# Taking even and odd chunks in turns in two small matrix products of an RWKV-7 block

## The chip, the cores and the metric

The kernel runs on one NeuronCore of a Trainium2 chip. The metric is the device time of one execution in microseconds (us). The kernel before was run three times: 3058.14, 3070.52 and 3070.98 us, with a median of 3070.52 us. A further execution, recorded by the hardware profiler, is what the profile below describes.

The engines are called as the profile calls them: PE is the matrix engine (PEld its weight loads), DVE the vector engine, ACT the scalar engine, POOL the GpSimd engine, SP the one that issues the DMAs. PSUM is the memory that PE writes its products into. A "stationary" operand is loaded into the array, a "moving" one streams through it.

## The reference: what is computed

A decoder block for 2048 tokens of width 1024 with two parallel branches, a causal convolution and RWKV-7 time mixing with 16 heads of width 64. The part that matters here is the RWKV-7 state, one 64 x 64 matrix a head, updated token by token:

```
def step(state, inp):
    r_t, w_t, k_t, v_t, kk_t, b_t = inp
    sk = jnp.einsum('bhvk,bhk->bhv', state, kk_t)
    state = (state * w_t[:, :, None, :] - sk[..., None] * b_t[:, :, None, :]
             + v_t[..., None] * k_t[:, :, None, :])
    return state, jnp.einsum('bhvk,bhk->bhv', state, r_t)
...
o = _rwkv7_scan(r, decay.reshape(hd), k, v, kk, kk * a)
o = _layernorm(o, gn_g.reshape(RWKV_HEADS, RWKV_HEAD), gn_b.reshape(RWKV_HEADS, RWKV_HEAD), GN_EPS)
```

Around it stand an input projection of width 9344, the convolution branch, two branch projections, sigmoid gates, an output projection and a final RMSNorm.

## The kernel before

**Tiling and stages.** The sequence is cut into 4 blocks (b) of 512 tokens. For each block the 16 heads are taken in 4 groups (g) of 4 heads; a group is two pairs (q) of two heads (hh). So there are 16 groups in all. The first 2531 us or so of the profile are these groups, with the input projections, the gates and the convolution laid between their steps; after that come the branch projections and the output.

**Chunks.** Inside a group the 512 tokens are cut into 8 chunks (c) of 64 tokens. A chunk's parity e = c % 2 decides which partitions its data live in, so that two chunks share one tile: `vrow(e)` is partitions 0 to 63 for an even chunk and 64 to 127 for an odd one, `prow(e)` the other half. `kcol` is `prow` and `rcol` is `vrow`. For each chunk and head the matrix `As` holds the products of keys and queries (L537, masked at L539); `uv` holds the values in the rows `vrow(e)`, and later the solved updates in the rows `prow(e)`.

**A group, in the source's order.**
- The two `pair` generators make decay factors, keys, queries and values (PE lines L505, L537, L552, L570; most of the rest of PE's time is the projections at L205).
- The values' part of x (L589 to L600): for each half c4 of the chunks (four chunks), a PSUM tile `aux` receives `As` times `uv` for four chunks and four heads. The stationary operand is 64 rows by 64 columns of `As`, the moving one 64 rows by 64 columns of `uv`, the output lies in the partitions `prow(e)`. Two copies on ACT (L600) move it to `XO`.
- The triangular inverse: blocks of `As` go to DRAM and come back as `La`, POOL makes the inverse in 31 steps (L624, L626), and it goes by DRAM back into `As`. DVE transposes parts of it (L652) for the products at L656 and L665.
- The recurrence over the 8 chunks: L683, L685 on DVE, L688 (four products of one chunk, 64 by 64, all in the partitions of that chunk's parity), L690 on DVE, L694, and L698 on DVE, which makes the next state.
- The last products of o (L700 to L713): again for each c4 a PSUM tile `late`, of which there is one, receives `As` times `uv` for four chunks and four heads. Here the stationary operand has all 128 rows and 64 columns, and the output lies in the partitions `vrow(e)`. These products are issued after the recurrence's last product. Two adds on DVE (L713) move the tile into `XO`.
- The normalisation of o and its store (L725 to L742). `XO` has one buffer.

**The order of the work.** The kernel is written with a tile framework that places semaphores, and lays out each engine's instructions with a simulated timeline (`schedule_with_timeline_sim=True`). The source's order gives the priority. So the last products of one group and the values' part of the next stand close together in PE's order, with projections between.

**How a product is recorded.** The operands are fp32, and the trace has two weight loads and two matmuls for each product written in the source; they are called passes here. At L596 and L708 there are 512 products each and 1024 passes.

**Another line of the same shape.** L505 (in `pair`) multiplies squared keys with columns of ones: for c in 0 to 7, a stationary operand of 128 rows by 64 columns and a moving one of 2 columns, into the partitions `prow(c % 2)`. Its parity changes with each product.

Of the kernel before, what the change touches and what calls it, by code (L numbers as in the profile page):

```python
# [82 lines left out]
def hybrid_block(ctx: ExitStack, tc: tile.TileContext, x, vecs, convk, w2a2, final_g, ada, w_in, w_co, w_ro, w_o, crow, out,  # L83
# [365 lines left out]
    def prow(e):  # L449
        return slice(64, 128) if e == 0 else slice(0, 64)  # L450

    def vrow(e):
        return slice(0, 64) if e == 0 else slice(64, 128)
# [121 lines left out]
    def group(b, g, h, lora, fill):  # L575
# [11 lines left out]
        for e in range(2):  # L587
            nc.gpsimd.memset(XO[vrow(e), e::2], 0.0)
        heads = [(q, hh) for q in range(2) for hh in range(2)]  # L589
        for c4 in range(NCH // 4):  # L590
            pv = pa.tile([P, 2, 2, P], F32, name="aux", tag="aux")
            for c in range(4 * c4, 4 * c4 + 4):
                e = c % 2
                for q, hh in heads:
                    hs = slice(64 * hh, 64 * hh + 64)
                    nc.tensor.matmul(pv[prow(e), c // 2 % 2, q, hs], As[q][vrow(e), hh, c, kcol(e)], uv[vrow(e), c, q, hs],  # L596
                                     start=(c // 2 % 2 == 0 and q == 0 and hh == 0), stop=(c // 2 % 2 == 1 and q == 1 and hh == 1),
                                     skip_group_check=True)
            for e in range(2):
                nc.scalar.copy(XO[prow(e), 4 * c4 + e:4 * c4 + 4:2], pv[prow(e)])  # L600
# [73 lines left out]
        for c in range(NCH):  # L674
            cc, e = c // 2, c % 2
# [25 lines left out]
        for c4 in range(NCH // 4):  # L701
            po = pl.tile([P, 2, 2, P], F32, name="late", tag="late")
            with tc.issue_after(last.ins if hasattr(last, "ins") else last):
                for c in range(4 * c4, 4 * c4 + 4):
                    e = c % 2
                    for q, hh in heads:
                        hs = slice(64 * hh, 64 * hh + 64)
                        nc.tensor.matmul(po[vrow(e), c // 2 % 2, q, hs], As[q][:, hh, c, rcol(e)], uv[:, c, q, hs],  # L708
                                         start=(c // 2 % 2 == 0 and q == 0 and hh == 0), stop=(c // 2 % 2 == 1 and q == 1 and hh == 1),
                                         skip_group_check=True)  # L710
            for e in range(2):
                sl = slice(4 * c4 + e, 4 * c4 + 4, 2)
                nc.vector.tensor_tensor(out=O[vrow(e), 2 * c4:2 * c4 + 2], in0=po[vrow(e)], in1=XO[vrow(e), sl], op=ALU.add)  # L713
# [158 lines left out]
    for b in range(NB):  # L872
        h = hprep(b) if b else hprep0(x0, ada_steps())
        lora = lora_split(h)
        for g in groups:
# [29 lines left out]

            wcount[0] = WSH
            group(b, g, h, lora, fill)
            if b == 0 and g == GG:
                for _ in ada_cols(srow, l3, "As", ASB, [((16 + k, 17 + k), (hgate_col[:, k:k + 1], hgate_col[:, k + 1:k + 2]))
# [247 lines left out]
```

## Time and profile before

| What | Value |
|---|---|
| Median of three runs | 3070.52 us |
| Lowest, highest | 3058.14, 3070.98 us |
| The profiled execution | 3056.37 us |
| Its span | 3054.7 us |
| Its mean granted clock of PE | 0.982 |
| Busy: PE, DVE, POOL, ACT | 95%, 67%, 41%, 33% |
| HBM traffic over the span | 226 GB/s |
| PE busy at L596, at L708 | 47.3, 49.8 us |

How to read it. A row of the groups by line gives line, engine, operation, `out<-in`, the array's rows and columns that are used (64*64), the moving operand's shape, the count, then the busy time in us and the mean duration of one instruction in ns, and after the second bar the idle time of the engine just before them with what ended it. A row of the timeline gives start and length in us of a run of like instructions, with the idle time before it in brackets. Ends of matmuls are modelled, and matmuls overlap, so the pace is read from starts: the length of a run less the length of one pass, over the number of steps. A row of the busy time by stretch gives the stretch, its length, then busy time and count of PE, PEld, DVE, ACT and POOL, the granted clock, the share of the DMA engines and GB/s. A row of the waits gives who waited for whom, us in total, times, and the longest.

### The profile page before, as it was taken

The page shows a single profiled execution, that of the slowest core. Times are in us where ns is not written, and L with a number is a line of the kernel's source. Part 1 is how long each engine was busy: PE and PEld are TensorE (multiplying, and loading weights), DVE is VectorE, ACT ScalarE, POOL GpSimd, SP SyncE. Part 2 cuts the span into 40 slices and gives each one's busy share as a digit, 9 for nine tenths or more (in the row PEclk, how much of TensorE's full clock was granted, in tenths as well). Part 3 has the DMA queues.
Part 4 walks back from the last instruction along what each step waited for, and adds up shares of the span by engine and source line. Part 5 has one row for each costly group of instructions (what it writes and reads, how often), then busy time and mean ns, then how long its engine had stood idle before and what let it go on. Part 6 is the DMA issues. An engine that isn't in the chain of part 4 may idle for free.

```text
span 3054.7 us, 64810 instructions
## 1 busy us (share of the span) xinstructions
PE 2911.1 (95%) x25672; PEld 2754.0 (90%) x25672; DVE 2045.2 (67%) x3879; ACT 1010.8 (33%) x1887; POOL 1257.3 (41%) x1788
## 2 busy tenths in 40 slices
PE   6789998999999999999999999999999999899998
PEld 5789898999999998999999998999999978687988
DVE  6676877686766675767677667667689534767333
ACT  4424344433333242324242424232332112333101
POOL 3445455533443435243434355426276004555000
PEclk9999999999999999999999999999999999999999
DMA  8666757774747477648585888646457687989674
GB/s 300 220 233 199 250 198 260 242 236 152 243 142 257 140 248 239 194 139 273 161 276 168 274 276 271 199 157 204 154 184 243 199 277 281 325 294 339 235 277 171
DMA packets 366367, 697.14 MB, mean 228 GB/s; under 512 B 135984, under 2 KB 154736, under 8 KB 366064
## 3 DMA queue, kind: packets, MB, share of 16 engines
q1 hardware_dynamic: 366064, 693.00, 67.9%
q8 instruction: 202, 3.31, 0.5%
q14 instruction: 101, 0.83, 0.1%
HBM read 504.04 MB, written 187.70 MB: 226 GB/s over the span
## 4 chain that ended last, share of the span: by engine, by line
PE 57%; DMA 15%; DVE 12%; POOL 7%; ACT 3%; issue 3%; SPq 2%; DVEq 0%; ACTq 0%; POOLq 0%
PE ps_main L205 40%; DMA w_st<-w_in_t 3%; PE aux L537 3%; DVE acc L774 2%; POOL TT L626 2%; POOL itmp L624 2%; DMA w_gr<-grow_d 2%; DMA w_st<-w_co_t 2%; PE xo L688 2%; PE pout L1078 2%; PE pout L1079 2%; PE pout L1077 2%; DMA w_st<-w_ro_t 1%; PE xo L683 1%; PE xo L694 1%
## 5 line engine op out<-in xcount | busy, mean ns | idle before, releaser
L205 PE MATMUL ps_main<-h_hi,w_hi 128*128 128x256 f32 x4608 | 953.4, 285 | 24.3 <-ACT w_hi L188 16.1
L205 PE MATMUL ps_main<-h_hi,w_lo 128*128 128x256 f32 x4608 | 955.6, 285 | 9.6 <-POOL w_lo L190 6.5
L205 PE MATMUL ps_main<-h_lo,w_hi 128*128 128x256 f32 x4608 | 953.4, 284 | 0.0
L205 PEld LDWEIGHTS ps_main<-h_hi,w_hi 128*128 128x128 f32 x4608 | 718.8, 190 | 33.7 <-ACT w_hi L188 17.3
L205 PEld LDWEIGHTS ps_main<-h_hi,w_lo 128*128 128x128 f32 x4608 | 718.2, 190 | 18.3 <-POOL w_lo L190 7.7
L205 PEld LDWEIGHTS ps_main<-h_lo,w_hi 128*128 128x128 f32 x4608 | 717.7, 190 | 4.8 <-issue 0.2
L774 DVE SCALAR_TENSOR_TENSOR acc<-u,ck,acc 128x512 f32<-128x512 f32 x928 | 698.0, 752 | 19.4
L624 POOL TENSOR_TENSOR itmp<-La,TT 128x126 f32<-128x126 f32 (+22 forms) x496 | 181.9, 367 | 126.7 <-DMA La<-dA 91.1
L626 POOL TENSOR_TENSOR TT<-TT,itmp 128x126 f32<-128x126 f32 (+22 forms) x496 | 190.1, 383 | 36.6
L190 POOL TENSOR_TENSOR w_lo<-w_st,w_hi 128x1024 fp32r<-128x1024 f32 x47 | 113.1, 2407 | 116.5 <-ACT w_hi L188 94.6
L680 ACT ACTIVATE Se<-S,pe 128x128 f32<-128x128 f32 x256 | 89.0, 395 | 198.0 <-DVE S L698 196.9
L537 PE MATMUL aux<-KR,BKz 128*128 128x128 f32 x1024 | 137.9, 283 | 12.4 <-POOL KR L523 6.2
L698 DVE TENSOR_TENSOR S<-xo,Se 64x128 f32<-64x128 f32 x256 | 73.5, 287 | 107.6 <-PE xo L694 96.9
L537 PEld LDWEIGHTS aux<-KR,BKz 128*128 128x128 f32 x1024 | 126.9, 197 | 14.9 <-POOL KR L523 6.8
L188 ACT CAST w_hi<-w_st 128x1024 fp32r<-128x1024 f32 x71 | 74.3, 1047 | 195.9 <-DMA w_st<-w_in_t 159.3
L690 DVE TENSOR_TENSOR uv<-xo,rn 64x256 f32<-64x256 f32 x128 | 53.8, 421 | 103.0 <-PE xo L688 101.6
L539 DVE TENSOR_TENSOR As<-aux,maskA 128x512 f32<-128x512 f32 x128 | 87.3, 687 | 38.4 <-PE aux L537 37.3
L685 DVE TENSOR_TENSOR XO<-xo,XO 128x256 f32<-128x256 f32 x128 | 53.7, 419 | 86.1 <-PE xo L683 70.1
L560 POOL TENSOR_TENSOR vv<-rk,vv 128x512 f32<-128x512 f32 x32 | 43.9, 1372 | 154.3 <-ACT rk L559 148.0
L754 ACT ACTIVATE th<-ps_main 128x512 f32<-128x512 f32 x64 | 38.1, 596 | 206.8 <-PE ps_main L205 150.1
L531 ACT COPY BKz<-BK 64x512 f32<-64x512 f32 x128 | 78.9, 616 | 62.7 <-PE aux L537 39.7
L786 ACT ACTIVATE th<-ps_main 128x512 f32<-128x512 f32 x64 | 38.1, 595 | 182.8 <-PE ps_main L205 172.7
(301 smaller groups left out, 5530.9 us busy)
## 6 DMA issues: line engine op xcount, KB each, us to landing
w_hi<-kh_in SPq DMA_DIRECT2D x219, 512.0 KB, 4.2
w_lo<-kl_in SPq DMA_DIRECT2D x219, 512.0 KB, 5.4
w_st<-w_in_t SPq DMA_DIRECT2D x73, 512.0 KB, 4.7
kh_in<-w_hi SPq DMA_DIRECT2D x71, 512.0 KB, 2.9
kl_in<-w_lo SPq DMA_DIRECT2D x71, 512.0 KB, 4.8
w_hi<-kh_ro SPq DMA_DIRECT2D x32, 512.0 KB, 5.1
w_lo<-kl_ro SPq DMA_DIRECT2D x32, 512.0 KB, 6.1
w_hi<-kh_co SPq DMA_DIRECT2D x32, 512.0 KB, 3.9
```

What stands on the lines that cost most here:

```text
L188: nc.scalar.copy(hi, st)
L190: lo_eng.tensor_tensor(out=lo, in0=st, in1=hi.bitcast(F32), op=ALU.subtract)
L205: nc.tensor.matmul(ps[:, qs], ww[:, k, :], aa[k][:, qs], start=(k == 0 and t == 0 and q == 0), stop=(k == KT - 1 and t == 2 and q == ms - ...
L531: nc.scalar.copy(BKz[hs, hh], BK[hs, c4 * 2:c4 * 2 + 2])
L537: nc.tensor.matmul(pA[:, c // 2, es], BKz[:, hh, c // 2, es], KR[:, cc, es], start=(c == 0), stop=(c == 3), skip_group_check=True)
L539: nc.vector.tensor_tensor(out=Asb[:, hh, c4 * 4:c4 * 4 + 4, :].rearrange("p (a e) n -> p a (e n)", e=2), in0=pA, in1=flat(maskA).unsqueeze ...
L624: nc.gpsimd.tensor_tensor(out=tmp[:, :ni, :nt], in0=La[:, j:j + 1, j + 1:].broadcast_to([P, ni, nt]), in1=TT[:, :ni, j:j + 1].broadcast_to ...
L626: nc.gpsimd.tensor_tensor(out=TT[:, :ni, j + 1:], in0=TT[:, :ni, j + 1:], in1=tmp[:, :ni, :nt], op=ALU.add)
L680: nc.scalar.mul(Se[:, q, :], Sg[:, q, :], R[q]["pe"][:, c:c + 1])
L688: nc.tensor.matmul(xo[pr_, q, hs], As[q][pr_, hh, c, kcol(e)], XO[pr_, c, q, hs], start=(q == 0 and hh == 0), stop=(q == 1 and hh == 1), s ...
L698: nc.vector.tensor_tensor(out=Sg[hs, :, hs], in0=xo[hs, 2:4, hs], in1=Se[hs, :, hs], op=ALU.add)
L774: nc.vector.scalar_tensor_tensor(out=acc if i + 1 < HALO else yj, in0=u[:, i:i + TB], scalar=ck[:, j, i:i + 1], in1=acc, op0=ALU.mult, op1 ...
```

## The change

In both places the four chunks of a PSUM tile were taken one after the other, each with its four heads. Now they are taken in two couples, an even chunk with the next odd one, and within a couple each head's product of the even chunk is followed by the same head's product of the odd chunk. The products themselves, their operands and their places are the same, and so are the conditions that start and stop the sums in PSUM.

```
+
+        def turns(c4):
+            return [(4 * c4 + 2 * a + e, q, hh) for a in range(2) for q, hh in heads for e in range(2)]
+
         for c4 in range(NCH // 4):
             pv = pa.tile([P, 2, 2, P], F32, name="aux", tag="aux")
-            for c in range(4 * c4, 4 * c4 + 4):
-                e = c % 2
-                for q, hh in heads:
+            for c, q, hh in turns(c4):
+                    e = c % 2
                     hs = slice(64 * hh, 64 * hh + 64)
                     nc.tensor.matmul(pv[prow(e), c // 2 % 2, q, hs], As[q][vrow(e), hh, c, kcol(e)], uv[vrow(e), c, q, hs],
                                      start=(c // 2 % 2 == 0 and q == 0 and hh == 0), stop=(c // 2 % 2 == 1 and q == 1 and hh == 1),
...
             with tc.issue_after(last.ins if hasattr(last, "ins") else last):
-                for c in range(4 * c4, 4 * c4 + 4):
-                    e = c % 2
-                    for q, hh in heads:
+                for c, q, hh in turns(c4):
+                        e = c % 2
                         hs = slice(64 * hh, 64 * hh + 64)
                         nc.tensor.matmul(po[vrow(e), c // 2 % 2, q, hs], As[q][:, hh, c, rcol(e)], uv[:, c, q, hs],
```

## The prediction

> **What bounds the kernel now.** I read the page first, then the groups by line, then the timeline around the two edited places, then the waits and the busy time by stretch. The page:
>
> ```profile
> span 3054.7 us, 64810 instructions
> PE 2911.1 (95%) x25672; PEld 2754.0 (90%) x25672; DVE 2045.2 (67%) x3879; ACT 1010.8 (33%) x1887; POOL 1257.3 (41%) x1788
> PE 57%; DMA 15%; DVE 12%; POOL 7%; ACT 3%; issue 3%; SPq 2%; DVEq 0%; ACTq 0%; POOLq 0%
> ```
>
> PE is busy for 95% of the span and idle for 143.6 us of it. PE time that is really saved should therefore mostly show in the end. The groups by line, with x products recorded as two passes each (16 groups of 8 chunks of 4 heads are 512 products, and the rows say x1024):
>
> ```profile
> L688 PE MATMUL xo<-XO,As 64*64 64x64 f32 x1024 | 90.0, 226 | 4.9 <-DVE XO L685 2.3 <-DVE carry L438 2.0 <-DVE As L670 0.6
> L708 PE MATMUL late<-uv,As 128*64 128x64 f32 x1024 | 49.8, 230 | 3.6 <-DVE XO L713 3.6
> L596 PE MATMUL aux<-uv,As 64*64 64x64 f32 x1024 | 47.3, 226 | 1.8 <-ACT tk L571 1.8
> L505 PE MATMUL aux<-bones,sq 128*64 128x2 f32 x512 | 23.3, 202 | 4.2 <-ACT sq L501 4.2
> ```
>
> The two edited lines, L596 (the values' part) and L708 (the last products of o), hold 97.1 us of PE. They are 3% of the span, so no gain can be large. What they could shrink to is read from how runs of them lie in time:
>
> ```profile
> 258.40 0.63 PE L505 MATMUL aux<-bones,sq 128*64 128x2 f32 x16
> 265.32 0.68 PE L688 MATMUL xo<-XO,As 64*64 64x64 f32 x8
> 292.18 1.54 PE L708 MATMUL late<-uv,As 128*64 128x64 f32 x32
> 296.27 2.69 PE L596 MATMUL aux<-uv,As 64*64 64x64 f32 x64 [1.77 <-ACT tk L571]
> ```
>
> One pass of these lasts 0.20 us at L505 and 0.22 us at the others (medians of 198, 218 and 222 ns, below). Taking that off a row's length gives the time from the first start to the last:
>
> ```profile
> L505 PE MATMUL aux<-bones,sq x512: 197/198/268, 73.4 to 2286.0; 128*64 128x2 f32 x171
> L688 PE MATMUL xo<-XO,As x1024: 218/218/366, 207.9 to 2516.4; 64*64 64x64 f32 x171
> L708 PE MATMUL late<-uv,As x1024: 222/222/368, 292.2 to 2530.9; 128*64 128x64 f32 x171
> ```
>
> - L688 is one chunk alone: its 8 passes all use the same half of the array's columns (prow of that chunk). From first to last start 0.46 us, or 66 ns a step.
> - L708 is 4 chunks, whose halves alternate by chunk: 1.32 us. Less one chunk's 0.46 that leaves 0.86 for three more chunks, 0.287 us each. L596 with 8 chunks agrees: 2.47 less 0.46, over 7, is 0.287.
> - A chunk needs 0.46 us, yet the next one begins 0.287 us after it. So two halves already work at the same time, but only partly: a half is left without work before its next chunk comes.
> - L505 has 16 passes that change half after every product, in the source (prow(c % 2) at each c): 0.43 us over 15 steps, 28.7 ns a step, which is 57 ns for each half with both always at work.
>
> So the present order runs at 36 ns a pass (0.287 over 8), and the nearest thing in this trace to the new order runs at 29.
>
> **The change part by part.** Both edits only permute products. The number of passes, the operands, the PSUM tiles, the evacuations and the DMAs stay. Of each PSUM half the first product still starts it and the last still stops it. No wait is added and no instruction on another engine moves in the source; the work that reads a run's result (the copies at L600, the adds at L713) needs all of it before and after.
>
> Step one, the pace. Let b be the step within a half that is always fed and a the first step of a half that had been left idle. From L505 b is 0.057 us; from L688, a + 6b = 0.46, so a is 0.118. In the new order a run of 32 passes gives 16 to each half: a + 14b = 0.92 us. Of 64 passes: a + 30b = 1.83 us.
>
> Step two, o. 32 runs of 32 passes, each 1.32 to 0.92: 0.40 us x 32 = **12.8 us**.
>
> Step three, the values. Whole runs of 64 go from 2.47 to 1.83, 0.64 us. Most groups are cut by the second half of o, as here:
>
> ```profile
> 630.06 2.11 PE L596 MATMUL aux<-uv,As 64*64 64x64 f32 x48
> 635.54 2.08 PE L708 MATMUL late<-uv,As 128*64 128x64 f32 x32 [3.37 <-DVE XO L713]
> 905.52 2.57 PE L596 MATMUL aux<-uv,As 64*64 64x64 f32 x62
> 908.02 1.54 PE L708 MATMUL late<-uv,As 128*64 128x64 f32 x32
> ```
>
> 62 passes go from 2.35 to 1.83, 48 passes from 1.89 to a + 22b = 1.37, both 0.52, and the remainders of 2 to 16 passes give a little. I take 0.6 us x 16 groups = **9.6 us**. PE is freed of 22.4 us in all.
>
> The alternated order with 64 moving columns is not in the trace, so its price has two ends. The good end is L505's 28.7 ns a pass, which gives the sum above; it has 2 moving columns where these have 64. The bad end is that a change of half always costs the first step a and nothing overlaps: a + b for two passes, 88 ns a pass. A run of 32 would take 2.7 us instead of 1.32 and one of 64 5.5 instead of 2.47, together 94 us more. I take the good end. L596 and L708 themselves, with 64 moving columns, run two halves side by side around each chunk's border, since 36 ns a pass is well under the 57 of one half. The far end I give 1 in 100.
>
> A page speaks against step two. The Trainium skill, "TensorE: Matmul & The Clock Gate", Part 3 ("The mechanism"), says that a weight load overlaps matmuls in flight only where the row groups differ. L708's two halves both use all 128 rows, so by it the sum would be the 9.6 us of step three. L505's row (128*64, 28.7 ns) and L708's own 0.287 us a chunk disagree with it.
>
> Step four, what comes through to the end. The busy time of three stretches, about a group long each, and PE's longest waits:
>
> ```profile
> 450.00:640.00 190.00, 176.98 (x1645) 171.91 (x1645) 140.62 (x238) 73.92 (x124) 106.18 (x154) 0.96 0.73 240
> 770.00:910.00 140.00, 140.00 (x1395) 136.23 (x1392) 98.87 (x194) 47.87 (x92) 61.38 (x107) 1.00 0.63 204
> 1367.00:1500.00 133.00, 133.00 (x1320) 129.21 (x1319) 92.90 (x185) 49.21 (x95) 54.60 (x91) 1.00 0.69 227
> ...
> PE ps_x L401 <- DVE dg L393: 18.9, 1, 18.9
> PE ps_main L205 <- ACT w_hi L188: 16.1, 4, 7.9
> PE xo L683 <- DVE S L698: 9.0, 7, 3.0
> ```
>
> The second column is PE's busy time. Some stretches have no PE idle time at all, and there 1.4 us less work (22.4 over 16 groups) is 1.4 us less time. In 450 to 640 PE waits 13 us; a wait that ends at a time set by a load or by POOL swallows what was saved just ahead of it. The 18.9 us lie at the start, before either line runs. The work that could come late next is the triangular inverse, which POOL and DMAs make while PE does other things. Here it had room:
>
> ```profile
> 798.34 0.49 DVE L652 STREAM_TRANSPOSE T<-As 32x128 f32<-32x128 f32 x2
> 809.16 2.11 PE L656 MATMUL late<-T,As 32*32 32x32 f32 x64
> ```
>
> PE takes up T 10.3 us after the last of it, against 1.4 us that are gained. For what waits swallow I take off about a tenth, 2.4 us, by choice: **20 us** come through.
>
> The profiled execution took 3056.37 us (span 3054.7), 14 us under the median of 3070.52 and close to the lowest of 3058.14. The sum gives 3036.4 for such an execution, and shifted to the median 3050.5.
>
> **The rivals.** *A: only the values' part gains*, because two column halves that share all rows do not go faster in turns at 64 moving columns. For it: L505 streams only 2 columns. Against it: L708's present overlap. It leaves 9.6 us, 8.6 of them at the end: 3061.9.
>
> *B: the waits swallow more than half.* The chain of waits gives PE only 57%, and 43% to DMA, DVE, POOL and others. With four tenths coming through, 9 us: 3061.5. Against it: stretches like 770 to 910.
>
> *C: the change doesn't do what it says.* The program is laid out by a scheduler with a simulated timeline, and it already splits L596 around L708 (48 or 62 of 64 passes stand ahead of the second half of o), so emitted order isn't source order. If it sorts the products back to a chunk at a time, nothing changes: 3070.5. Against it: in the rows each run stands whole otherwise.
>
> *D, slower: the second half of o stands at its PSUM tile.* There is one such tile, so the second 32 products of o need both adds of L713 done, and those queue on DVE behind whatever stands there:
>
> ```profile
> 633.69 0.30 DVE L652 STREAM_TRANSPOSE T<-As 32x128 f32<-32x128 f32 x1 [5.08 <-DMA As<-dT]
> 634.00 1.39 DVE L713 TENSOR_TENSOR XO<-late,XO 64x512 f32<-64x512 f32 x2
> 905.05 1.39 DVE L713 TENSOR_TENSOR XO<-late,XO 64x512 f32<-64x512 f32 x2
> L652 DVE STREAM_TRANSPOSE T<-As 32x128 f32<-32x128 f32 x128 | 35.6, 292 | 71.7 <-DMA As<-dT 70.2
> ```
>
> At 634 DVE stood 5.08 us for the inverse's DMA with the adds behind it, and PE stood 3.37 us, with all its later work behind that. What covers the adds is the values' run between the two halves of o, which the change shortens by about 0.5 us. If each of 16 groups stood 3.37 us: 53.9, less the 3.6 that L708 waits now, less 22.4, is 28 us more: 3098. It is slower by over 0.5% from 2.6 us a group on ((22.4 + 3.6 + 15.4) / 16). Against it: at 905 the adds end at 906.44 and o resumes at 908.02, 1.58 us spare, of which 0.5 goes; and only 3.6 us of such waits exist now.
>
> **How the numbers follow.** Forecast 0.62, A 0.07, B 0.14, C 0.07, D 0.09, the far end of the price 0.01. About 0.5% (15 us) is what a measurement of this kernel can tell from no change. The forecast lies beyond it: faster 0.62. A, B and C stay within: same 0.28. D and the far end: slower 0.10. The range reaches down to 3034, which is all 22.4 us off the lowest run with 2 us of the present stalls gone as well, and up to 3073, no gain at the highest run (3070.98) and 2 us over. It leaves out D and the far end. The forecast's own range is 3035 to 3058, the upper end with 12.5 us coming through at the median.
>
> **What would show it.** Right: runs of 32 at L708 last about 1.14 us instead of 1.54, runs of 64 at L596 about 2.05 instead of 2.69, and PE's busy time falls by about 22 us to 2889. L708 at 1.5 with L596 shorter is A. Both unchanged is C. Both shorter with PE's idle time up by more than 10 us is B, and if the increase stands at L708 <- DVE XO L713, it is D. A run of 32 over 1.54 us would make the prediction wrong at its root, in the pace.

## The result, and the profile after

The changed kernel takes 3089.53 us (median of 6 runs, 3081.93 to 3094.28), the kernel before 3068.15 us beside it (median of 6, 3058.14 to 3070.98). The ratio is 1.0080, with a 95% interval of 1.0062 to 1.0098 (the two medians alone give 1.0070, inside it): slower by 0.8%, where 0.65% faster was forecast, and outside the range.

The profiled executions lie further apart than the medians: 3056.37 us before is under all 6 timed runs, 3094.28 after is the longest of its 6. So the 37.8 us between the two spans are some 16 us more than the 21.4 between the medians. The page of the kernel after, in the lines that were shown of before (its last line follows a chain that reaches back only to 1984 us, so its shares add up to a third and can't be held against those of before):

```profile
span 3092.5 us, 64846 instructions
PE 2916.4 (94%) x25672; PEld 2755.7 (89%) x25672; DVE 2059.9 (67%) x3879; ACT 1011.0 (33%) x1887; POOL 1252.6 (41%) x1788
PE 23%; DVE 5%; DMA 2%; POOL 2%; issue 2%; SPq 0%; ACT 0%; POOLq 0%; DVEq 0%; ACTq 0%
```

PE is busy for 5.3 us more than before, and idle for 176.1 us (3092.5 less 2916.4) where it was 143.6. Neither the work at the edited lines nor its pace explains that. The groups by line:

```profile
L691 PE MATMUL xo<-XO,As 64*64 64x64 f32 x1024 | 89.6, 226 | 2.1 <-DVE XO L688 1.3 <-DVE As L673 0.6
L710 PE MATMUL late<-uv,As 128*64 128x64 f32 x1024 | 37.7, 228 | 4.4 <-DVE XO L715 4.4
L599 PE MATMUL aux<-uv,As 64*64 64x64 f32 x1024 | 36.0, 221 | 2.2 <-ACT tk L571 2.2
L505 PE MATMUL aux<-bones,sq 128*64 128x2 f32 x512 | 23.8, 203 | 3.2 <-ACT sq L501 3.2
```

L710 (L708 before) fell from 49.8 to 37.7 us, L599 (L596 before) from 47.3 to 36.0. Together that is 23.4 us less; the forecast had 22.4. The runs in the timeline of the kernel after:

```profile
293.24 1.15 PE L710 MATMUL late<-uv,As 128*64 128x64 f32 x32
295.65 2.08 PE L599 MATMUL aux<-uv,As 64*64 64x64 f32 x64 [0.50 <-ACT tk L571]
```

They last 1.15 and 2.08 us; 1.14 and 2.05 were forecast. The 28.7 us that PE's busy time gained elsewhere (5.3 plus 23.4) lie mostly in passes that did not change. One of the three groups of the projections, before and then after (the three together gained 23.8 us):

```profile
L205 PE MATMUL ps_main<-h_lo,w_hi 128*128 128x256 f32 x4608 | 953.4, 284 | 0.0
```

```profile
L205 PE MATMUL ps_main<-h_lo,w_hi 128*128 128x256 f32 x4608 | 962.5, 286 | 0.0
```

The same 4608 passes take 9.1 us more, and PE ran longer at a lower clock: the mean granted clock is 0.973 in place of 0.982. The records of the two executions show full or half clock only, so that is 167 us at half clock (2 x 0.027 x 3092.5) against 110. At L205 two passes start every 0.24 us at full clock and every 0.43 us at half (in the timeline of the kernel after, around 1987 and 2002 us), so by estimate some 26 of the 57 us more are added PE time. But the profiled execution of before had an unusually high clock. Its executions beside the runs below had 0.979 in the mean (0.975 to 0.982), the six of the change 0.973 (0.970 to 0.977). That is about 37 us more at half clock, and by the same estimate 17 us of PE time. How such a stretch begins is shown below.

What PE waits for, of the kernel before and then of the kernel after, in rows that grew:

```profile
PE xo L694 <- DVE uv L690: 4.5, 4, 2.1
PE late L739 <- POOL XO L734: 1.7, 2, 0.9
PE late L656 <- DVE T L652: 1.0, 4, 0.3
```

```profile
PE xo L697 <- DVE uv L693: 12.3, 10, 3.0
PE ps_main L205 <- DMA w_hi<-kh_in: 7.1, 3, 4.4
PE late L659 <- DVE T L655: 6.8, 6, 2.5
PE late L741 <- POOL XO L736: 5.0, 5, 1.3
PE late L710 <- DVE XO L715: 4.4, 2, 3.9
PE late L741 <- POOL TT L622: 3.3, 1, 3.3
```

(L697, L659 and L741 are L694, L656 and L739 before, which has no wait for w_hi from kh_in in its list.) No single wait took the time. Several small ones grew, others shrank (L683, now L686, on S went from 9.0 to 2.2). Those at T, at XO and behind POOL's TT, 12 us more together, hang on the inverse or on POOL's queue. The largest increase, at uv, is a wait for DVE, and it stays when the inverse is shorter (below). The wait of rival D, L710 on the adds at L715, went from 3.6 to 4.4 us.

The other thing that differs is the order of all the work. The edit permutes 16 products within a PSUM tile. The scheduler laid out the whole program anew: in PE's order 5962 of 21782 places hold a product for a tile of another name than before, the first of them at place 1778. It also moved work on the other engines.

**What the new order does around the inverse.** One group's way from its key and query products (L537) to the inverse and back to PE, the 13th of 16, in the timeline of the kernel before:

```profile
1915.59 1.95 PE L537 MATMUL aux<-KR,BKz 128*128 128x128 f32 x16
1929.71 0.24 POOL L624 TENSOR_TENSOR itmp<-La,TT 128x31 f32<-128x31 f32 x1 [5.73 <-DMA La<-dA]
1943.57 2.57 PE L596 MATMUL aux<-uv,As 64*64 64x64 f32 x62
1958.45 0.25 POOL L626 TENSOR_TENSOR TT<-TT,itmp 128x16 f32<-128x16 f32 x1
1970.08 0.49 DVE L652 STREAM_TRANSPOSE T<-As 32x128 f32<-32x128 f32 x2 [3.94 <-DMA As<-dT]
1978.70 2.11 PE L656 MATMUL late<-T,As 32*32 32x32 f32 x64
```

The inverse starts 13.9 us ahead of the values' part (1929.71 to 1943.57), and PE takes up T 8.6 us after the first transpose, with all 64 passes in one run. The same group of the kernel after:

```profile
1934.87 1.50 PE L537 MATMUL aux<-KR,BKz 128*128 128x128 f32 x12
1947.40 1.61 PE L599 MATMUL aux<-uv,As 64*64 64x64 f32 x48
1951.17 0.24 POOL L627 TENSOR_TENSOR itmp<-La,TT 128x31 f32<-128x31 f32 x1 [8.99 <-DMA La<-dA]
1981.92 0.25 POOL L629 TENSOR_TENSOR TT<-TT,itmp 128x16 f32<-128x16 f32 x1
1991.52 1.10 DVE L655 STREAM_TRANSPOSE T<-As 32x128 f32<-32x128 f32 x4 [5.78 <-DMA As<-dT]
1991.88 0.69 PE L659 MATMUL late<-T,As 32*32 32x32 f32 x16 [1.92 <-DVE T L655]
```

The last passes of L537 now end 11 us ahead of the values' part and not 26, and the inverse starts 3.8 us behind that part. PE is at L659 before T is there and takes the 64 passes in pieces of 16, 8, 32 and 8 as T comes, with projections between. The same two differences, worked out for some groups (counted from 0; room is the time from the first transpose to the first product with T):

| Group | Inverse's start against the values' part, before | after | Room before | after |
|---|---|---|---|---|
| 0 | +10.2 us | +9.8 | 0.4 us | 0.4 |
| 5 | -13.9 | -3.6 | 19.6 | 8.5 |
| 8 | -18.5 | +0.4 | 21.6 | 3.2 |
| 9 | -13.5 | -2.7 | 20.0 | 6.5 |
| 11 | -32.3 | -11.4 | 26.3 | 7.0 |
| 12 | -13.9 | +3.8 | 8.6 | 0.4 |
| 13 | -0.5 | 0.0 | 0.8 | 0.5 |
| 14 | +1.7 | +2.4 | 0.5 | 1.5 |

Little room is not yet a wait: PE's 6.8 us of idle time at T all lie in the groups 12, 13 and 14 (2.3, 2.8 and 1.7 us; before, 0.8 and 0.2 in 13 and 14). In the groups 0, 8, 9 and 11 PE did not idle there.

And the busy time by stretch around the wait of group 12, in the kernel after (columns as before; the last three are granted clock, DMA share and GB/s):

```profile
1991.50:1994.50 3.00, 2.28 (x32) 2.00 (x33) 2.58 (x7) 0.00 (x0) 0.21 (x1) 1.00 0.19 30
1994.50:2004.70 10.20, 10.20 (x77) 9.62 (x76) 7.75 (x14) 0.60 (x1) 0.00 (x0) 0.50 0.54 178
2004.70:2010.00 5.30, 5.30 (x93) 5.13 (x91) 2.86 (x7) 0.00 (x0) 0.00 (x0) 0.99 0.49 167
```

After idle times of 1.92 and 0.34 us PE worked without a gap for 10.2 us at half clock. By the estimate above that costs another 4.6 us, which the profile books as busy time.

### The profile page after: what moved, and what is told of

It is laid out like the page before. It is cut to its first block, busy times and chain, and to the rows that moved or that the text cites. A ratio compares the mean times of both kernels' runs of the same rounds, so it can differ in the third digit from the quotient of the medians.

```text
span 3092.5 us, 64846 instructions
## 1 busy us (share of the span) xinstructions
PE 2916.4 (94%) x25672; PEld 2755.7 (89%) x25672; DVE 2059.9 (67%) x3879; ACT 1011.0 (33%) x1887; POOL 1252.6 (41%) x1788
## 5 line engine op out<-in xcount | busy, mean ns | idle before, releaser
L205 PE MATMUL ps_main<-h_hi,w_hi 128*128 128x256 f32 x4608 | 960.7, 287 | 37.3 <-ACT w_hi L188 18.7
L205 PE MATMUL ps_main<-h_hi,w_lo 128*128 128x256 f32 x4608 | 963.0, 286 | 10.4 <-POOL w_lo L190 6.2
L205 PE MATMUL ps_main<-h_lo,w_hi 128*128 128x256 f32 x4608 | 962.5, 286 | 0.0
L205 PEld LDWEIGHTS ps_main<-h_hi,w_hi 128*128 128x128 f32 x4608 | 725.0, 192 | 49.2 <-ACT w_hi L188 20.1
L205 PEld LDWEIGHTS ps_main<-h_hi,w_lo 128*128 128x128 f32 x4608 | 725.1, 191 | 18.4 <-POOL w_lo L190 7.4
L205 PEld LDWEIGHTS ps_main<-h_lo,w_hi 128*128 128x128 f32 x4608 | 724.2, 191 | 5.9
L683 ACT ACTIVATE Se<-S,pe 128x128 f32<-128x128 f32 x256 | 89.0, 394 | 185.3 <-DVE S L701 184.0
L537 PE MATMUL aux<-KR,BKz 128*128 128x128 f32 x1024 | 135.5, 281 | 10.5 <-ACT BKz L531 4.5
L537 PEld LDWEIGHTS aux<-KR,BKz 128*128 128x128 f32 x1024 | 125.6, 195 | 12.7 <-ACT BKz L531 4.9
L788 ACT ACTIVATE th<-ps_main 128x512 f32<-128x512 f32 x64 | 38.2, 596 | 208.7 <-PE ps_main L205 197.7
L688 DVE TENSOR_TENSOR XO<-xo,XO 128x256 f32<-128x256 f32 x128 | 53.8, 420 | 70.2 <-PE xo L686 59.3
L432 ACT ACTIVATE t<-ps_main,mu 128x512 f32<-128x512 f32 x96 | 65.6, 684 | 83.2 <-PE ps_main L205 74.7
L951 POOL TENSOR_TENSOR ot<-ot,bt 128x512 f32<-128x512 f32 x24 | 35.4, 1478 | 140.0 <-DMA bt<-bv_d 139.9
```

The lines of the kernel that those rows point to most:

```text
L205: nc.tensor.matmul(ps[:, qs], ww[:, k, :], aa[k][:, qs], start=(k == 0 and t == 0 and q == 0), stop=(k == KT - 1 and t == 2 and q == ms - ...
L432: nc.scalar.activation(t1, ps, AF.Identity, scale=mu1[:, mi:mi + 1])
L537: nc.tensor.matmul(pA[:, c // 2, es], BKz[:, hh, c // 2, es], KR[:, cc, es], start=(c == 0), stop=(c == 3), skip_group_check=True)
L683: nc.scalar.mul(Se[:, q, :], Sg[:, q, :], R[q]["pe"][:, c:c + 1])
```

## The experiments

Three theories stood against one another. **Turns:** the turns themselves cost time. **Order:** the turns bring what they should, and the new order of the program loses more. **Waits:** PE time freed at these lines is not on the path, whatever the order.

To part them, products were put into another order after the scheduler had done its work, at the 16 places that a tile's products hold, so that no engine's order changes otherwise:

```
+def turned():
+    return [(2 * a_ + e, q, hh) for a_ in range(2) for q in range(2) for hh in range(2) for e in range(2)]
+def chunked():
+    return [(c, q, hh) for c in range(4) for q in range(2) for hh in range(2)]
...
+        for run in RUNS:
+            names = {k: i.ins.name for k, i in run.items()}
...
+            for n, k in zip(sorted(at[x] for x in names.values()), order):
+                ins[n] = old[at[names[k]]]
```

All ratios below are to the kernel before on the same chip, with 95% intervals. A per cent is 30.7 us.

### Turns and order taken apart

Before's order, the products in turns (in e3 the values' part alone, in e4 o alone):

```
+    relaid(nc, turned())
```

> Every engine's instructions stand as in the kernel before; only the 16 products of each PSUM tile at L596 and L708 change places among themselves, into the change's order. If the scheduler's new layout is what cost the time (layout theory), this is 18 to 23 us under the kernel before (ratio 0.993), with L708 near 37.7 us and L596 near 36.0 us of PE. If taking turns itself brings a cost elsewhere, such as a lower granted clock (turns theory), it is about 20 us over the kernel before (ratio 1.007), as the change is.

> The layout of the kernel before, turns only in the values' part (L596). By the sum of the prediction 9.6 us less PE and about 9 us less time (ratio 0.997); if waits swallow the saving, no change.

> The layout of the kernel before, turns only in the last products of o (L708). By the sum 12.8 us less PE and about 12 us less time (ratio 0.996). By rival A (column halves that share all 128 rows gain nothing) no change and L708 at 49.8 us.

Measured: 0.9989 (0.9971 to 1.0007) for both lines, 0.9992 (0.9976 to 1.0007) for the values, 0.9976 (0.9961 to 0.9991) for o. The groups by line of the first:

```profile
L708 PE MATMUL late<-uv,As 128*64 128x64 f32 x1024 | 37.7, 228 | 5.4 <-DVE XO L713 5.4
L596 PE MATMUL aux<-uv,As 64*64 64x64 f32 x1024 | 37.1, 222 | 1.1 <-ACT tk L571 1.1
```

The turns are as quick here as in the change, 22.3 us less than before, and the kernel gains only 3.5. That refutes the theory of turns, and also the half of the theory of order by which the turns bring what they should; it bears out that of waits for before's order. The products of o alone brought 7.4 us of their 12, clear of noise; the two lines together did not bring more. Held against before instruction by instruction, in the same order, its trace (the longest of its 12 executions) has waits longer by 0.7 to 3.4 us at 21 places and shorter by 0.7 to 1.7 us at 11, 16.5 us more idle time in sum. They are spread over KR and XO (POOL), T, th and mr (DVE), sq, rk and BKz (ACT). Part of the saving goes into the clock: 0.978 in the mean over its 12 executions against 0.979, by estimate 5 us of PE time.

The change's own order, the products put back a chunk at a time:

```
+    relaid(nc, chunked())
```

> Every engine's instructions stand as in the changed kernel, but the 16 products of each PSUM tile go back to a chunk at a time. Layout theory: it keeps the layout's cost and loses the saving, so about 23 us over the changed kernel and 43 us over the kernel before (ratio 1.014). Turns theory: near the kernel before (ratio 1.000).

Measured: 1.0052 (1.0030 to 1.0075), 3084.94 us. The order by itself costs 16 us, and not the 43 that the theory of order expected. With the turns in it the change has 1.0080; the two intervals overlap, so whether the turns cost anything more in this order isn't settled.

### Whether PE's time is on the path

In before's order, a chunk at a time, 190 of the 13824 passes of the wide projections at L205 left out, among those that carry no wait and no signal, about 22 us of PE:

```
+    if ms == 2 and (k, t) == (3, 1) and CALLS[0] // 2 % 3 == 0:
+        RUNS.append(mm)
...
+        new = [i for i in old if not (i.name in gone and quiet(i))]
```

> The kernel before, in its layout and with its chunk order, with 190 of the 13824 passes of the projections at L205 left out (one correction term of every third projection, two passes each), 22 us of PE spread over the groups. It asks what PE time is worth anywhere. If the other engines and the loads are just in time behind PE (theory of waits), little comes through, as with the turns: 4 to 8 us (ratio 0.998). If PE is the bound and the turns have a cost of their own, about 20 us come through (ratio 0.993).

Measured: 1.0004 (0.9988 to 1.0020). Twenty-two microseconds less of the engine that is busy for 95% of the span are worth 4 us at most by the interval. The clock takes part here too: 0.977 in the mean against 0.980, by estimate 7 us of PE time. Next, six of the 30 taps of the convolution at L774 cut from 512 columns to 8 (their part of the convolution is left out; DVE is busy for 95 us less), with the products a chunk at a time (e7) and in turns (e8):

```
-            nc.vector.scalar_tensor_tensor(out=acc if i + 1 < HALO else yj, in0=u[:, i:i + TB],
+            mm = nc.vector.scalar_tensor_tensor(out=acc if i + 1 < HALO else yj, in0=u[:, i:i + TB],
...
+    TAPS.extend([mm] * (10 <= i < 16))
```

> The kernel before, in its layout and with its chunk order; 6 of the convolution's 30 accumulating taps at L774 are cut from 512 columns to 8, so their part of the convolution is left out for the other columns: 192 instructions, some 120 us less of DVE, PE's work unchanged. If it is DVE's queue that PE waits for, 10 us or more under the kernel before (ratio below 0.997); if the waits stand elsewhere, no change.

> The same cut of the convolution's taps, together with the turns at L596 and L708, in the layout of the kernel before. If DVE's queue is what swallows the turns' saving, it now comes through: 15 to 20 us under the run with fewer taps alone. If not, about 4 us under it, as the turns bring in the old layout.

Measured: 0.9999 (0.9984 to 1.0015) and 0.9971 (0.9953 to 0.9989). DVE's load alone is worth nothing that can be measured; with turns on top there may be a little more than with turns alone, within the intervals.

The other way round: the first product of each tile issued four times in place of once, 192 products more:

```
+            if i.name in first:
+                for t in range(times):
+                    new.append(copy.replace(i, name=f"I-{4000000 + n}", sync_info=None))
```

> Before's order on every engine and its products a chunk at a time, but the first product of each of the 64 PSUM tiles is issued four times in place of once: 192 further products, 384 passes in the rhythm of one chunk, about 22 us more of TensorE's time at the two lines of the change, and no more work on any other engine. The theory that TensorE is only one of several engines that are just in time for one another (22 us less of it elsewhere were worth nothing) leaves two cases. If the other engines set the pace and TensorE has room: 3067 to 3073 us, ratio 1.000 to 1.002. If TensorE stands just on the edge, so that time taken from it is given back as waits and time given to it lengthens the path: 3084 to 3092 us, ratio 1.005 to 1.008. The forecast's own step, that this time is on the path at full length, wants the second too, and it is told from the second case by the runs with less of TensorE alone.

```profile
L708 PE MATMUL late<-uv,As 128*64 128x64 f32 x1216 | 60.5, 227 | 1.2 <-DVE XO L713 1.2
L596 PE MATMUL aux<-uv,As 64*64 64x64 f32 x1216 | 57.8, 223 | 0.0
```

The two lines take 21.2 us more than before (60.5 and 57.8 against 49.8 and 47.3), and the kernel 9.8: 1.0032 (1.0018 to 1.0045), between the two cases. PE stands at the edge. More of it costs about half its length; less of it brought between nothing (22 us at L205) and 7 us (12 us at o).

### Whose chain it runs into

Before's order again, POOL's two operations in each of the first 28 steps of the inverse narrowed to 2 columns, which leaves part of the inverse out (it has 31 steps); with turns (e12), and without (e14):

```
-            nc.gpsimd.tensor_tensor(out=tmp[:, :ni, :nt], in0=La[:, j:j + 1, j + 1:].broadcast_to([P, ni, nt]),
+            m1 = nc.gpsimd.tensor_tensor(out=tmp[:, :ni, :nt], in0=La[:, j:j + 1, j + 1:].broadcast_to([P, ni, nt]),
...
+    CUT.extend([m1, m2] * (j < 28))
```

> Before's order with the products in turns, and GpSimd's two operations of each of the first 28 steps of the 32-step inverse narrowed to two columns: that part of the inverse is left out, so that GpSimd ends each inverse sooner; no engine's order changes. If it is GpSimd's chain (the inverse, then KR, RK and XO on its queue) that TensorE runs into when the turns let it be early, the turns' saving comes through: about 3043 to 3050 us, ratio 0.992 to 0.9945. If the waits that take the saving's place come from VectorE and ScalarE as well, or from products that wait for one another's copies: 3058 to 3065 us, ratio 0.997 to 0.9995, as with the turns alone.

> Before's order, its products a chunk at a time, and only GpSimd's two operations of each of the first 28 steps of the inverse narrowed to two columns (that part of the inverse is left out). Theory that GpSimd's inverse alone sets the pace where TensorE waits, so that the turns could bring nothing: nearly the whole gain of the kernel with both, 3046 to 3054 us, ratio 0.993 to 0.996. Theory that TensorE and GpSimd are both just in time, so that neither alone is worth much and only both together: 3060 to 3067 us, ratio 0.9975 to 0.9995, and the turns are then worth 13 to 20 us on top of it, against 4 us without it.

Measured: 0.9937 (0.9919 to 0.9955) with turns, 0.9975 (0.9963 to 0.9986) without. The inverse's groups, in the kernel before and in the one with turns:

```profile
L626 POOL TENSOR_TENSOR TT<-TT,itmp 128x126 f32<-128x126 f32 (+22 forms) x496 | 190.1, 383 | 36.6
L624 POOL TENSOR_TENSOR itmp<-La,TT 128x126 f32<-128x126 f32 (+22 forms) x496 | 181.9, 367 | 126.7 <-DMA La<-dA 91.1
```

```profile
L626 POOL TENSOR_TENSOR TT<-TT,itmp 128x16 f32<-128x16 f32 (+15 forms) x496 | 120.3, 243 | 36.6
L624 POOL TENSOR_TENSOR itmp<-La,TT 128x16 f32<-128x16 f32 (+15 forms) x496 | 117.0, 236 | 124.7 <-DMA La<-dA 89.1
```

POOL is freed of 135 us at these lines, 8 us a group. The inverse itself becomes shorter by less, since it also waits: from its first operation to its last it takes 27.9 us in place of 28.9 in group 5 (e14). That alone brings 7.7 us, the turns alone 3.5, both together 19. On top of the short inverse the turns are worth 12 us (0.9975 to 0.9937). So the likelier reading is that PE and POOL are both just in time and neither is the bound alone. The excess of the two together over the sum is 8 us, about as much as the intervals leave open.

The change itself with the short inverse:

> The change as it is, in the order that the scheduler gave it, with GpSimd's inverse narrowed in the same way (that part of the inverse is left out). If what the change's own order costs is GpSimd's chain met more often: 3043 to 3055 us, ratio 0.992 to 0.996, the same as before's order with turns and the short inverse (0.9937). If the order costs by something else (waits on VectorE's copies and weights, and the low clock behind them): the short inverse takes off as much as it does in before's order with turns, about 16 us, and no more, 3068 to 3078 us, ratio 1.000 to 1.0035.

Measured: 0.9939 (0.9925 to 0.9954), 3048.41 us. That is 43 us under the change (1.0080) and the same as before's order with turns and the short inverse (0.9937). The same narrowing takes 16 us off before's order with turns (0.9989 to 0.9937), 43 off the change's. So all of what the change's order costs, 28 us against the same turns in before's order (1.0080 less 0.9989; 8 us either way by the intervals), goes when POOL has less to do at the inverse. Its page, its waits, and the stretch that answers to the one of group 12:

```profile
span 3050.9 us, 64846 instructions
PE 2903.0 (95%) x25672; PEld 2746.2 (90%) x25672; DVE 2052.0 (67%) x3879; ACT 1011.8 (33%) x1887; POOL 1117.1 (37%) x1788
```

```profile
PE xo L697 <- DVE uv L693: 11.2, 10, 2.7
PE late L659 <- DVE T L655: 2.1, 3, 0.8
PE late L741 <- POOL XO L736: 1.3, 2, 0.7
```

```profile
1956.00:1976.00 20.00, 19.39 (x248) 18.00 (x247) 15.34 (x29) 0.60 (x1) 0.21 (x1) 1.00 0.56 171
```

PE's idle time is back at 147.9 us (176.1 in the change), the waits at T and XO have shrunk from 6.8 and 5.0 to 2.1 and 1.3, and in this stretch PE keeps the full clock where it had run at half. Over all six executions the clock is 0.979, as before. The wait at uv, which had grown most, is still 11.2 us, so it isn't where the price was paid.

The room at T did not come back, though: the groups 8, 9, 11 and 12 have 3.7, 9.3, 5.4 and 0.4 us here, against 3.2, 6.5, 7.0 and 0.4 in the change. In group 12 the inverse takes 26.7 us in place of 31.0, and PE reaches T 41.3 us after the start of the values' part in place of 44.5. So the room in the table shows how the new order differs, and not by itself what it costs. The lead over the change grows all along: the last product of o comes 5 us sooner in group 2, 19 in group 8, 29 in group 11, 42 in group 13 and 45 in group 15.

The same, with the inverse shortened in some of the 16 groups only (part of the inverse left out there): six with at most 7 us of room, and the other ten. (The expectation speaks of all such groups; group 0, with 0.4 us both before and after, is among the ten.)

```
-    gone, n = {i.ins.name for i in CUT}, 0
+    gone, n = {i.ins.name for k, i in enumerate(CUT) if k // 56 in (8, 9, 11, 12, 13, 14)}, 0
```

> The change in its own order, with GpSimd's inverse narrowed to two columns in its first 28 steps in six of the 16 groups only, those in which it ends at most 7 us before TensorE needs it (that part of the inverse is left out there). All 16 narrowed gave 0.9939, none gave 1.008. If the order's price is paid at the inverses that TensorE waits for: most of the 41 us, 3053 to 3065 us, ratio 0.9955 to 0.999. If a shorter inverse helps alike wherever it is: six sixteenths of 43 us, 16 us, 3070 to 3077 us, ratio 1.001 to 1.003.

> The same in the other ten groups only. If the order's price is paid at the inverses that TensorE waits for: 3073 to 3084 us, ratio 1.002 to 1.0055. If a shorter inverse helps alike wherever it is: ten sixteenths of 43 us, 27 us, 3059 to 3066 us, ratio 0.9975 to 0.9995.

Measured: 0.9990 (0.9973 to 1.0006) for the six, 28 us off; 1.0028 (1.0013 to 1.0044) for the ten, 16 us off. The parts add up to the whole, 44 and 43. One of the six groups brings 4.6 us, one of the ten 1.6. In before's order with turns the narrowing brings 16 us, 1 us a group if it is shared evenly. By that estimate 22 of the 28 us of the price hang on POOL's work in these six groups, among them the three where PE waits for T, and 6 on the ten. Which of POOL's results is met late there isn't shown. Nor is it shown that POOL alone has this effect, since the run with less DVE work was made in before's order only.

### Other orders

The same turns with the odd chunk first, which the scheduler lays out in a third way, and that order with the products a chunk at a time:

```
-            return [(4 * c4 + 2 * a + e, q, hh) for a in range(2) for q, hh in heads for e in range(2)]
+            return [(4 * c4 + 2 * a + 1 - e, q, hh) for a in range(2) for q, hh in heads for e in range(2)]
```

> The changed kernel with the odd chunk's product ahead of the even one's: the same turns at the same pace, but the scheduler lays the instructions out in a third way. If only turns as such cost time, it is like the change, some 20 us over the kernel before (ratio 1.007). If each layout has a time of its own, it lies elsewhere, from 15 us under to 30 us over the kernel before.

> The order that the scheduler gave the kernel with the odd chunk first (0.9968 of before) stays as it is on every engine, and the 16 products of each of the 64 PSUM tiles are put back a chunk at a time at the places that they hold there, so that no products share the array in turns. Theory of the layout (each order of the whole program has a time of its own, within about half a per cent either way, and the turns are worth about 4 us in any): about 3 to 6 us over the kernel with the odd chunk first, 3061 to 3065 us, ratio 0.998 to 0.9995; the order by itself is then no worse than before's. Theory of the turns (the 23 us of TensorE that they save come through where the order leaves room for them, and in the third order they do): about 3075 to 3082 us, ratio 1.003 to 1.005. Theory that the order is all and the turns nothing: 3057 to 3060 us, ratio 0.9965 to 0.998.

Measured: 0.9968 (0.9950 to 0.9986), 3058.66 us, for the odd chunk first; 0.9992 (0.9980 to 1.0003) with its products a chunk at a time. Here the turns are worth 7 us, give or take as much, and the order costs nothing. The room in it is much as before: 23.1, 19.9, 27.6 and 5.6 us in the groups 8, 9, 11 and 12.

Turns in the source for one of the two places alone, the other a chunk at a time (e13 and e19: the values' part, e16: o). The edit against the change, of e13; e16 has it at the values' part:

```
+        def chunks(c4):
+                return [(4 * c4 + 2 * a + e, q, hh) for a in range(2) for e in range(2) for q, hh in heads]
...
-                for c, q, hh in turns(c4):
+                for c, q, hh in chunks(c4):
```

> In the source, turns for the values' part alone (a product of an even chunk and of the next odd one in turns), the products of o a chunk at a time; the scheduler lays out the whole program anew, and TensorE's order differs from before's at 3768 of 21782 places. The same edit in before's order gave 0.9992. Theory of the layout (any edit of this kind draws an order, whose time lies within about half a per cent either way, whatever the edit): away from 0.9992 by some 0.1 to 0.5 per cent in a direction that cannot be told, 3052 to 3083 us, ratio 0.995 to 1.005. Theory that the turns themselves cost time with an even chunk first: slower by about half of what the change of both lines was, 3076 to 3082 us, ratio 1.003 to 1.005. If the order is worth nothing: 3063 to 3067 us, ratio 0.9985 to 1.000.

> In the source, turns for o alone, the values' part a chunk at a time; the scheduler lays out the whole program anew, with TensorE's order differing from before's at 2414 of 21782 places (5962 for the change, 3768 for the turns of the values' part alone). The same edit in before's order gave 0.9976, the two lines edited together gave 1.008 and the values' part alone 1.0031. If an order's price grows with how far it differs: 0.997 to 1.001, 3058 to 3070 us. If each drawn order has a price of its own that cannot be told ahead: anywhere from 0.994 to 1.008. If the price belonged to the values' part (its turns make the scheduler start something late), o alone costs nothing: 0.996 to 0.9985, 3055 to 3063 us.

> Turns of the values' part alone in the source, in the order that the scheduler gave it (1.0031), with the inverse narrowed in all 16 groups (that part of the inverse is left out). If this order's price too is paid at the inverse: 3050 to 3058 us, ratio 0.9945 to 0.997, near before's order with the same turns and a short inverse. If it is paid elsewhere: 3064 to 3071 us, ratio 0.999 to 1.001, less by 8 to 12 us than with the whole inverse.

Measured: 1.0031 (1.0020 to 1.0042) for the values' part alone, 0.9967 (0.9952 to 0.9983) for o alone, and 0.9968 (0.9953 to 0.9983) for the values' part with the short inverse (part of the inverse left out). The values' part in before's order had 0.9992, so this order too has a price, 12 us. The short inverse takes off 19 us here; in before's order it takes off 7.7 without turns and 16 with both. So it is not settled whether this price goes in the same way: before's order with turns of the values alone and the short inverse was not run. In the trace of e13 the room at T in the groups 8 to 12 is as before, and its 5.0 us of waits at T lie in the groups 13 and 14, so where its price is paid stays open. Orders whose PE places differ from before's at 2235 (odd first), 2414 (o alone), 3768 (values alone) and 5962 (the change) gave 0.9968, 0.9967, 1.0031 and 1.0080. Four orders are too few for a rule.

The kernels with the odd chunk first and with turns for o alone beat both the kernel before and the change: 10 us under before, over 30 under the change.

## Why the prediction was wrong

**Steps one to three, the pace, were right.** a and b from L688 and L505 gave 12.8 and 9.6 us; L710 lost 12.1 and L599 11.3 (in before's order 12.1 and 10.2). For 62 passes a + 29b is 1.77 us where the sum has 1.83, which is a small slip on the same side. The row of 2 moving columns told the price for 64. So rival A is out, and the far end too. On A's page the trace decides: the Trainium skill, "TensorE: Matmul & The Clock Gate", Part 3 ("The mechanism"), has weight loads overlap only where row groups differ, and L710, whose two halves share all rows, went from 49.8 to 37.7 us.

**Step four failed, in two ways.**

- That *"no instruction on another engine moves in the source"* is true, and it was taken to mean that nothing else moves. Rival C knew that a scheduler with a simulated timeline lays out the program, but drew from it only that the products might be sorted back. That the layout of all other work could change was a term put at nothing without a reason. This is the larger part: 28 us, from 0.9989 to 1.0080, and 16 us with the products a chunk at a time. No row of the profile told which way a layout would go: the one with the odd chunk first costs nothing.
- *"PE time that is really saved should therefore mostly show in the end"* doesn't hold here. Even with nothing else moved, 3.5 of 22.3 us came through, and 22 us less at L205 brought nothing that could be measured. The tenth taken off for waits should have been over four fifths (three fifths at least, by the interval). The busy share of 95% hid that PE meets its partners nearly just in time: of what was freed, later waits took most and a lower clock a part.

**The check of the inverse looked at one group.** The row at 798.34 had 10.3 us of room after the last transpose shown there (15.8 after the first, the count of the table), and that was held against the 1.4 us gained there. Among the 16 groups of the same trace three had 0.4, 0.8 and 0.5 us (groups 0, 13 and 14). And the inverse loads POOL's queue in every group, which the room at T doesn't show.

**The rivals.** B named the mechanism that holds in before's order (0.9989; it priced 0.9971), but not the result. C was wrong as put: the turns are in the trace. D had the right sign and the wrong place: L710's wait on L715 came to 4.4 us and not 54. **What would show it** pointed the right way: both runs shorter, with PE's idle time up by 32.5 us, was to be B or D. A new layout was not on its list.

What stays open: why the scheduler put L537 nearer to the values' part; which of POOL's results, T, XO or others, PE meets late in the change's order; how the 16 us that the ten other groups bring are shared; and where the values' part alone, in its own order, pays its 12 us.

## What to carry to other kernels

Where a scheduler lays out the program, first compare the order of every engine before and after: an edit that only permutes can move a quarter of PE's places, and its own worth is known only with the rest held still. Read the room of the nearest partner in every repetition of the loop, not in one, and test it by shortening the partner: in this kernel little room alone did not show where the time went. And before putting a saving on the path at full length, take as much work away somewhere else on that engine; if the time doesn't move, expect little of the saving.

## What the runs showed of the hardware

- Two column halves that share all 128 rows work side by side when products alternate: 32 passes of 64 moving columns last 1.15 us, 30 ns a pass (1.15 less 0.22, over 31), against 43 ((1.54 less 0.22) over 31) a chunk at a time.
- A short lull can cost more than itself. Idle times of 1.92 and 0.34 us were followed by 10.2 us at half clock under full load. The Trainium skill, "TensorE: Matmul & The Clock Gate", in the part "HAM oscillation — how this bites in real kernels", warns of idle gaps over about 3.4 us; here less was enough. Not every such lull does it: before, PE idled 1.77 us ahead of L596 at 296.27, and the clock stayed full from 290 to 310 us. Between the two profiled executions, before and after, the time at half clock grew from 110 to 167 us.
- A narrow operation on POOL is not cheap: with 28 of the 31 steps narrowed to 2 columns (by 1 to 14 rows), so from 92 elements a partition in the mean to 16, the mean of the inverse's operations fell only from 383 to 243 ns and from 367 to 236.
